# An SBUF-to-SBUF copy and transposes of the rounded type for the scaled attention scores

## The chip, the core and the metric

The kernel runs on one core of one Trainium2 chip. The metric is the device time of one execution in microseconds (us), as the median of several runs. Engines are named as in the profile: PE (TensorE, matrix products and transposes), PEld (its weight loads, which overlap PE), DVE (VectorE), ACT (ScalarE), POOL (GpSimd), SP (SyncE, which here only issues transfers). SBUF is the memory on the core, 128 partitions wide; PSUM holds the results of PE; DRAM is the large memory outside.

## What is computed

The reference is one layer of an encoder for two sequences (prompt and sample) of 1024 rows by 1024 columns, in fp32. The change lies in its attention part. Cut to that and its neighbours:

```python
h = rmsnorm(x, g_mix) * (1.0 + sc1) + sh1
z = h @ w_in                                   # 256 q_lat, 128 kv_lat, 64 k_pe, 512 f_in
q = (rmsnorm(q_lat, g_q_lat) @ w_uq)           # 4 heads of 128 + 64
q_pe, k_pe = apply_rope(q_pe), apply_rope(k_pe)
sc = (qn @ k_nope.T + q_pe @ k_pe.T) * scale   # per head, 1024 x 1024
p = jax.nn.softmax(sc, axis=-1)
y_mla = p @ v
mix = jnp.concatenate([y_mla, y_four], axis=-1) @ w_out
x = x + ga1 * mix
h2 = rmsnorm(x, g_ffn) * (1.0 + sc2) + sh2
ffn = (jax.nn.silu(h2 @ w_gate) * (h2 @ w_up)) @ w_down
out = rmsnorm(x + ga2 * ffn, g_final)
```

`y_four` is a Fourier mixing of the 512 columns of `f_in`. It is done before attention begins.

## The kernel before, in words

**Arithmetic.** An fp32 product is made of three products in the rounded type F32R (the trace prints `fp32r`). `split` (L61 to L63) turns a tile into a rounded high part (ACT, L62) and the rest (DVE, L63). `mm3` (L82 to L85) multiplies high by high, high by low and low by high. A plain fp32 tile can go through PE as well, which the kernel does only for transposes. A transpose on PE is a product with a 128 x 128 identity matrix: `ident` in fp32, `identr` in the rounded type. `rd(t)` (L58) reads the bits of a rounded tile as fp32.

**Stages.** Up to about 300 us of the span run the modulation, the input projection and the Fourier part. From 300 to 722 us runs attention (L1175 to L1338), and from there to the end the feed-forward part with products of the Strassen kind (`bank` in the profile). The rest of this section is on attention.

**Items.** Attention is cut into 64 items (s, b, h, u): 2 sequences, 4 blocks of 256 queries, 4 heads, 2 halves of 128 queries. Eight items make a block. Item k runs like this:

1. PE makes the scores of 128 queries against 1024 keys (`scores`, L1186 to L1200) into `ps_s`, two PSUM tiles of 1024 columns: for each 512 columns three products of the absorbed query `qa` with the latent keys `lat` (L1191 to L1193), and products with the rotary query `qp` (L1194, L1199, L1200).
2. DVE takes the maximum of each row (L1206, `mx`) and multiplies it by the negative scale (L1207, `nb`).
3. ACT takes the exponential from PSUM into the SBUF tile `p` (L1209), with the sum of each row.
4. DVE takes the reciprocal of the sum (L1210, `rr`) and scales `p` in place (L1211).
5. In the next item's turn PE turns `p` (`flip_p`, L1215 to L1226): eight transposes of 128 x 128 (L1225) in two groups of four, each group into one PSUM tile `ppt`. ACT and DVE split it into `pt`.
6. After every fourth item `values` (L1228) multiplies `pt` by the values `ckv`, 24 products, for two heads.

Between these stand, for the block ahead: `load_q` (L819, loads `ql`), `rope_q` (L834, the rotary query, with a temporary of 512 columns from `half`, L808, tag "hv"), `rope_flip` (L855, its transposes in the rounded type at L858), `absorb_q` (L863, the absorbed query `qa`, from `qa_tiles`, L831). And for the block behind: `out_load` (L1117, loads the tile `x2`, which the profile prints as `x`), `out_proj` (L1123, 12 products for 512 columns of output), `norm2` (L1132: stores `x2`, squares it on ACT, makes the reciprocal root `rs_r` on POOL by `rstd`, L100, and scales on DVE at L1143 into `xn`), `flip_h` (L1150: transposes of `xn` at L1157 into `pht`, shift and scale on ACT at L1160, and a store of `ht` at L1162).

**Memory.** A tile of a pool is given a number of buffers by `bufs`; the next tile of that tag waits until the one that many tiles ago is no longer read. Before the change `p` has three buffers, `qa` three, `hv` two. The PSUM tiles of the transposes (`tbank`, L1114: `ppt`, `pht`, `pqt`) share two.

**Order.** The Python code says what is done item by item (the loop from L1290 on, with `todo`, L1283, for the smaller steps). The framework's scheduler then sets the order of each engine, by its own estimates, so one more instruction in a chain can move others on every engine. Each engine goes through its list in order: an instruction that waits holds up all behind it.

**Transfers.** SP issues the loads and most stores of this stage, in one list: `ql`, `lat`, `ckv`, `x2`, `ht`, and at the change of sequence, items 34 to 38, the gate `gah` (L1244, in `gate_half`) and the weights `wvr` (L1269, in `wv_load`), which POOL multiplies by the gate (L1270). POOL issues transfers that add into DRAM (`add_x`, L798). When attention ends the next stage loads its input `H` from DRAM (L1366 and L1376), issued by SP as well.

Of the kernel before, what the change touches and what calls it, by code (L numbers as in the profile page):

```python
# [12 lines left out]
F32 = mybir.dt.float32  # L13
F32R = mybir.dt.float32r
# [7 lines left out]
P = 128  # L22
D = 1024
N = 1024
# [28 lines left out]
def hybrid_encoder_kernel(ctx: ExitStack, tc: tile.TileContext, a: dict):  # L53
    nc = tc.nc
# [3 lines left out]
    def rd(t):  # L58
        return t.bitcast(F32)

    def split(hi, lo, src):  # L61
        here["a"] = nc.scalar.copy(hi, src).ins  # L62
        here["v"] = nc.vector.tensor_tensor(out=lo, in0=src, in1=rd(hi), op=ALU.subtract).ins  # L63
# [27 lines left out]
    ident = const.tile([P, P], F32, name="ident")  # L91
    make_identity(nc, ident)
    identr = const.tile([P, P], F32R, name="identr")
# [81 lines left out]
    with ExitStack() as st:  # L175
        p1b = st.enter_context(ExitStack())
        w2 = p1b.enter_context(tc.tile_pool(name="p1b", bufs=1, side="right", reuse_waits="tile"))
        w = st.enter_context(tc.tile_pool(name="p1", bufs=1, reuse_waits="tile"))
# [617 lines left out]
    S = {}  # L796
# [9 lines left out]
            nc.gpsimd.dma_start(fo_d[s][bs, gs], xs[s][bs, gs], accum_op=ALU.add)  # L806

    def half(name):  # L808
        return e.tile([P, 512], F32, tag="hv", name=name, bufs=2)

    def load_seq(s, lat):
        ckv = [e.tile([P, 8, KVL], F32R, tag=f"ckv{i}", name=f"ckv{i}", bufs=1) for i in range(2)]
# [16 lines left out]
        return e.tile([P, HEADS, P], F32R, tag="qp", name="qp", bufs=4)  # L829

    def qa_tiles():  # L831
        return [e.tile([P, 256], F32R, tag=f"qa{i}", name=f"qa{i}", bufs=3) for i in range(2)]

    def rope_q(s, b, u, bankf):  # L834
        ql = S["q", s, b]
# [27 lines left out]
    def absorb_q(s, b, h, bankf):  # L863
        ql = S["q", s, b]
        pq = bankf()
        hs = slice(h * P, h * P + P)
        for c in range(2):
            mm3(pq[:, :256], wq_h[:, c, hs], wq_l[:, c, hs], ql[0][:, c, :], ql[1][:, c, :], c == 0, c == 1)
        qa = qa_tiles()
        split(qa[0], qa[1], pq[:, :256])  # L870
        S["qa", s, b, h] = qa

    def stage3_loads():
        wq_h = e.tile([P, 2, 768], F32R, name="wq_h")
        wq_l = e.tile([P, 2, 768], F32R, name="wq_l")
        half("hv")
        rc = e.tile([P, 8, ROPE], F32, name="rc")
        rs = e.tile([P, 8, ROPE], F32, name="rs")
        lat = [e.tile([P, 2, N], F32R, tag=f"lat0{i}", name=f"lat0{i}") for i in range(2)]
        sk_tile()  # L880
        load_q(0, 0)
        for c in range(2):
            wqr = e.tile([P, 768], F32, tag=f"ckv{c}", name="wqr", bufs=1)
            nc.sync.dma_start(wqr, wq_d[:, c])
            split(wq_h[:, c, 512:768], wq_l[:, c, 512:768], wqr[:, 512:768])
            split(wq_h[:, c, 0:512], wq_l[:, c, 0:512], wqr[:, 0:512])
        qa_tiles()
        nc.sync.dma_start(rc, a["ropec"])
        nc.sync.dma_start(rs, a["ropes"])
        load_seq(0, lat)  # L890
        return wq_h, wq_l, rc, rs

    with ExitStack() as st:
        early = st.enter_context(ExitStack())
        wa = early.enter_context(tc.tile_pool(name="p2a", bufs=1, reuse_waits="tile"))
        w = st.enter_context(tc.tile_pool(name="p2", bufs=1, side="right", reuse_waits="tile"))
# [175 lines left out]
        for s in range(2):  # L1072
            for n in range(8):
                g, j = n // 4, (1, 2, 3, 0)[n % 4]
# [14 lines left out]
                if s == 1 and n == 0:  # L1089
# [3 lines left out]
                    e = E3.enter_context(tc.tile_pool(name="p3e", bufs=1, side="left", reuse_waits="tile"))  # L1093
# [20 lines left out]
    def tbank(name, dt=F32):  # L1114
        return tl_ps.tile([P, 4, P], dt, tag="t", name=name, bufs=2)
# [59 lines left out]
    with ExitStack() as st:  # L1175
        w = st.enter_context(tc.tile_pool(name="p3", bufs=1, side="right", reuse_waits="tile"))
# [3 lines left out]
        def score_bank():  # L1180
            return pp.tile([P, N], F32, tag="s", name="ps_s", bufs=2)

        def scores(s, b, h, u):
            lat = S[s][0]
            qa, qp = S["qa", s, b, h], S["qp", s, b, u]
            us = slice(u * P, u * P + P)  # L1186
            ps = score_bank() if u == 0 else S.pop("ps")
            for g in range(2):
                gs = slice(512 * g, 512 * g + 512)
                o = ps[:, gs]  # L1190
                nc.tensor.matmul(o, qa[0][:, us], lat[0][:, 0, gs], start=u == 0, stop=False)  # L1191
                nc.tensor.matmul(o, qa[0][:, us], lat[1][:, 0, gs], start=False, stop=False)
                nc.tensor.matmul(o, qa[1][:, us], lat[0][:, 0, gs], start=False, stop=False)  # L1193
                nc.tensor.matmul(o, qp[:, h, :], lat[0][:, 1, gs], start=False, stop=u == 1)  # L1194
            if u == 0:
                pn, qn = score_bank(), S["qp", s, b, 1]
                for g in range(2):
                    gs = slice(512 * g, 512 * g + 512)
                    nc.tensor.matmul(ps[:, gs], qp[:64, h, :], lat[1][:64, 1, gs], start=False, stop=True)  # L1199
                    nc.tensor.matmul(pn[:, gs], qn[64:, h, :], lat[1][64:, 1, gs], start=True, stop=False)  # L1200
                S["ps"] = pn
            mx = tiny.tile([P, 1], F32, name="mx")
            nb = tiny.tile([P, 1], F32, name="nb")
            sm = tiny.tile([P, 1], F32, name="sm")
            rr = tiny.tile([P, 1], F32, name="rr")
            nc.vector.tensor_reduce(out=mx, in_=ps, axis=AX.X, op=ALU.max)  # L1206
            here["nb"] = nc.vector.tensor_scalar(out=nb, in0=mx, scalar1=-SCALE, scalar2=None, op0=ALU.mult).ins  # L1207
            p = w.tile([P, N], F32, tag="p", name="p", bufs=3)
            here["exp"] = nc.scalar.activation(p, ps, AF.Exp, bias=nb, scale=SCALE, accum_out=sm).ins  # L1209
            nc.vector.reciprocal(rr, sm)  # L1210
            nc.vector.tensor_scalar(out=p, in0=p, scalar1=rr[:, 0:1], scalar2=None, op0=ALU.mult)  # L1211
            S["p", s, b, h, u] = p
            S["rr"] = rr

        def flip_p(s, b, h, u):  # L1215
            p = S.pop(("p", s, b, h, u))
            if h % 2 == 0 and u == 0:
                S["pt", s, b, h // 2] = [[w.tile([P, 4, 4, P], F32R, tag=f"pt{k}{g}", name=f"pt{k}{g}", bufs=1) for k in range(2)]
                                         for g in range(2)]
            i = 2 * (h % 2) + u  # L1220
            for g in range(2):
                pth, ptl = S["pt", s, b, h // 2][g]
                pt = tbank("ppt")
                for c in range(4):
                    nc.tensor.transpose(pt[:, c, :], p[:, (4 * g + c) * P : (4 * g + c + 1) * P], ident)  # L1225
                split(pth[:, :, i, :], ptl[:, :, i, :], pt)  # L1226

        def values(s, b, q):  # L1228
            ckv = S[s][1]
# [66 lines left out]
        for k in range(nit + 4):  # L1296
            if k >= nit:
                i = k - nit
# [5 lines left out]
            if k < nit:  # L1304
                s, b, h, u = items[k]
                scores(s, b, h, u)
                if "scale" in S:
                    with tc.issue_after(here["nb"]):
                        S.pop("scale")()
                if k == nit - 1:  # L1310
                    with tc.issue_after(here["exp"]):
                        nc.scalar.activation(tiny.tile([P, 1], F32, tag="pc", name="warm"), cmask[:, 0:1], AF.Silu)
                nxt = items[k + 8 - k % 8] if k + 8 - k % 8 < nit else None
                i = k % 8
                if nxt is not None:
                    if i == 0:
                        load_q(*nxt[:2])
                    if i == 3 and nxt[1] == 0:
                        load_seq(nxt[0], [w.tile([P, 2, N], F32R, tag=f"lat1{i}", name=f"lat1{i}") for i in range(2)])
                    if i in (3, 4):  # L1320
                        rope_q(*nxt[:2], i - 3, gbank)
                    if i in (5, 6):
                        rope_flip(*nxt[:2], i - 5, tbank("pqt", F32R))
                if u == 1 and k + 1 < nit:
                    absorb_q(*items[k + 1][:3], gbank)
# [4 lines left out]
            if 0 <= k - 1 < nit:  # L1330
                flip_p(*items[k - 1])
                if k == nit:
                    S["tail"] = here["a"], here["v"]
# [6 lines left out]
    with ExitStack() as st:  # L1340
        w = st.enter_context(tc.tile_pool(name="p5", bufs=1, reuse_waits="tile"))
# [170 lines left out]
        for s in range(2):  # L1512
# [243 lines left out]
            def first_squares(half, t, v):  # L1756

                m[half, t] = tiny.tile([P, 2], F32, name=f"ms_{half}")
                me[half, t] = tiny.tile([P, 1], F32, name=f"me_{half}")
                jk = val()  # L1760
                nc.scalar.activation(jk, v, AF.Square, scale=1.0 / 32.0, accum_out=m[half, t][:, 0:1])
                nc.gpsimd.tensor_scalar(out=me[half, t], in0=m[half, t][:, 0:1], scalar1=EPS, scalar2=None, op0=ALU.add)
# [217 lines left out]
```

## Time and profile before

| | before |
|---|---|
| time, median of 3 runs | 2027.19 us (2027.05 to 2034.22) |
| time of the profiled execution | 2031.3 us |
| its span in the trace | 2029.5 us |
| instructions in the trace | 28291 |
| busy of PE, 0 to 300 us | 283.69 of 300 us |
| busy of PE, 300 to 722 us (attention) | 412.87 of 422 us |
| busy of PE, 722 to 2029 us | 1287.65 of 1307 us |
| mean granted clock of PE | 0.994 |

The profile is of one execution. Its times in the trace count from the start of the span. In a row of the timeline stand the start, the time that the group of like instructions took (for a group of several, from the first to the end of the last), the engine, the line of the kernel, the operation, its tiles as "out <- in", the shape, and the count; a bracket at the end holds the time that the engine idled ahead of it and what it waited for. In the groups, "busy, mean ns of one" is followed by the idle time ahead of the group and what ended it. Durations of products on PE overlap, since a product starts while the one ahead drains; how fast PE gets on is read from the starts. SPq and POOLq are the lists of transfers of SP and POOL.

### The profile page before, as it was taken

To read this page: it belongs to the slowest core of one execution; us is meant where nothing else is said; L and a number is where in the kernel's file an instruction comes from. 1 tells how busy PE (TensorE), PEld (TensorE's weight loads), DVE (VectorE), ACT (ScalarE), POOL (GpSimd) and SP (SyncE) were. 2 spreads that over 40 slices of the span, in tenths; PEclk is the share of its full clock that TensorE was granted. 3 is DMA by queue.
4 is the path that set the end of the run, shared out by engine and by line. 5 is a ranking of instruction groups with operands and counts; after the bars stand their busy time and mean duration, and the time that the engine had idled before them with its cause. 6 is when DMAs were issued, how large, how long until landed. Compare 5 with 4: busy or idle time off the path is not lost.

```text
span 2029.5 us, 28291 instructions
## 1 busy us (share of the span) xinstructions
PE 1984.2 (98%) x9840; PEld 1624.1 (80%) x9840; DVE 1407.3 (69%) x2088; ACT 896.9 (44%) x1733; POOL 830.1 (41%) x1013
## 2 busy tenths in 40 slices
PE   8899999999999999999999999999999999999997
PEld 7788877888777777888888888877788888888876
DVE  5667757766677679878677577687755655657674
ACT  4555545555555564333333365453333333336441
POOL 2454123112313227879779411233654555510142
PEclk9999999999999999999999999999999999999999
DMA  9685793445542575645655587674422322357662
GB/s 376 207 289 171 255 346 102 125 94 130 138 122 94 178 269 187 207 163 192 206 166 190 178 304 249 219 234 147 141 93 102 116 93 103 116 184 270 229 224 89
DMA packets 181963, 370.33 MB, mean 182 GB/s; under 512 B 18556, under 2 KB 58236, under 8 KB 177724
## 3 DMA queue, kind: packets, MB, share of 16 engines
q1 hardware_dynamic: 163148, 310.71, 45.8%
q0 software_dynamic: 18672, 57.81, 9.5%
q8 instruction: 77, 1.26, 0.3%
q14 instruction: 66, 0.54, 0.1%
HBM read 256.46 MB, written 120.39 MB: 186 GB/s over the span
## 4 chain that ended last, share of the span: by engine, by line
PE 54%; DVE 2%; DMA 2%; POOL 1%; issue 1%; ACT 1%; SPq 0%; DVEq 0%; ACTq 0%; POOLq 0%
PE bank L84 18%; PE bank L83 18%; PE bank L85 18%; DVE wl L63 1%; DMA draw<-s_d 1%; POOL val L143 1%; DVE val L143 1%; ACT wh L62 0%; DMA val<-x_d 0%; DMA draw<-t_d 0%; DVE val L1777 0%; POOL rs_y L110 0%; DMA rgu<-in_wgu_dram 0%; DVE val L1751 0%; DVE val L140 0%
## 5 line engine op out<-in xcount | busy, mean ns | idle before, releaser
L83 PE MATMUL bank<-H,wh 128*128 128x512 f32 x1224 | 477.3, 390 | 5.1 <-DVE val L143 5.1
L85 PE MATMUL bank<-H,wl 128*128 128x512 f32 x1224 | 476.3, 389 | 0.2 <-DVE wl L63 0.2
L84 PE MATMUL bank<-H,wh 128*128 128x512 f32 x1224 | 476.2, 389 | 0.0
L143 DVE TENSOR_TENSOR val<-bank,val 128x512 f32<-128x512 f32 x244 | 166.8, 688 | 169.9 <-PE bank L85 167.2
L83 PEld LDWEIGHTS bank<-H,wh 128*128 128x128 f32 x1224 | 229.8, 188 | 55.6 <-DVE val L143 7.0
L85 PEld LDWEIGHTS bank<-H,wl 128*128 128x128 f32 x1224 | 229.8, 188 | 49.2 <-DVE wl L63 1.1
L84 PEld LDWEIGHTS bank<-H,wh 128*128 128x128 f32 x1224 | 229.8, 188 | 47.3
L63 DVE TENSOR_TENSOR wl<-draw,wh 128x512 fp32r<-128x512 f32 x286 | 201.3, 739 | 83.0 <-ACT wh L62 82.4
L62 ACT CAST wh<-draw 128x512 fp32r<-128x512 f32 x286 | 168.6, 621 | 157.9 <-PE bank L84 86.8
L84 PE MATMUL bank<-wl,wh 128*128 128x512 f32 x572 | 223.6, 391 | 2.5 <-DVE wl L63 2.5
L143 POOL TENSOR_TENSOR val<-val 128x512 f32<-128x512 f32 x58 | 83.1, 1441 | 344.9 <-DVE val L1751 188.7
L85 PE MATMUL bank<-wh,wl 128*128 128x512 f32 x572 | 222.6, 389 | 0.0
L83 PE MATMUL bank<-wh 128*128 128x512 f32 x572 | 222.6, 389 | 0.0
L62 ACT CAST wh<-rgu 128x512 fp32r<-128x512 f32 x171 | 106.5, 624 | 249.1 <-PE bank L84 193.8
L63 DVE TENSOR_TENSOR wl<-val,wh 128x512 fp32r<-128x512 f32 x133 | 132.4, 997 | 75.5 <-ACT wh L62 75.4
L63 DVE TENSOR_TENSOR wl<-rgu,wh 128x512 fp32r<-128x512 f32 x171 | 168.1, 984 | 5.8 <-ACT wh L62 5.8
L62 ACT CAST wh<-val 128x512 fp32r<-128x512 f32 x133 | 82.4, 623 | 178.7 <-PE bank L84 162.8
L140 POOL TENSOR_TENSOR val<-rgu 128x512 f32<-128x512 f32 x80 | 113.1, 1414 | 96.4 <-DMA rgu<-in_wgu_dram 92.6
L84 PEld LDWEIGHTS bank<-wl,wh 128*128 128x128 f32 x572 | 107.4, 188 | 27.7 <-DVE wl L63 5.5
L83 PEld LDWEIGHTS bank<-wh 128*128 128x128 f32 x572 | 107.4, 188 | 22.7 <-ACT wh L62 0.2
L85 PEld LDWEIGHTS bank<-wh,wl 128*128 128x128 f32 x572 | 107.4, 188 | 21.7
L140 POOL TENSOR_TENSOR val<-val 128x512 f32<-128x512 f32 x89 | 119.4, 1358 | 1.3
(393 smaller groups left out, 3919.9 us busy)
## 6 DMA issues: line engine op xcount, KB each, us to landing
rgu<-in_wgu_dram SPq DMA_DIRECT2D x86, 512.0 KB
draw<-s_d SPq DMA_DIRECT2D x143, 256.0 KB
s_d<-val POOLq DMA_DIRECT2D x88, 256.0 KB, 3.9
draw<-t_d SPq DMA_DIRECT2D x88, 256.0 KB
s_d<-val SPq DMA_DIRECT2D x66, 256.0 KB
wada<-in_wa_dram SPq DMA_DIRECT2D x16, 1024.0 KB
draw<-in_w_down_dram SPq DMA_DIRECT2D x55, 256.0 KB
xt<-in_x_dram SPq DMA_DIRECT2D x16, 512.0 KB
```

The costliest lines, as they stand in the source:

```text
L62: here["a"] = nc.scalar.copy(hi, src).ins
L63: here["v"] = nc.vector.tensor_tensor(out=lo, in0=src, in1=rd(hi), op=ALU.subtract).ins
L83: nc.tensor.matmul(out, lh, rh, start=first, stop=False, skip_group_check=cont)
L84: nc.tensor.matmul(out, lh, rl, start=False, stop=False, skip_group_check=cont)
L85: here["pe"] = nc.tensor.matmul(out, ll, rh, start=False, stop=last, skip_group_check=cont).ins
L140: return eng.tensor_tensor(out=out, in0=x, in1=y, op=ALU.subtract).ins
L143: return eng.tensor_tensor(out=out, in0=x, in1=y, op=ALU.add).ins
```

## The change

Three tags lose a buffer: `hv` goes from two to one, `qa` from three to two, `p` from three to two. A new tile `pr` of the same size as `p`, of the rounded type and with two buffers, is filled from `p` by a transfer that SP issues after the scaling (`rd(pr)` makes it a copy of bits, so nothing is rounded in it). The eight transposes read `pr` with `identr` and write PSUM tiles declared in the rounded type, whose bits `split` reads as fp32. Two lines are added, so the transposes stand at L1227 in the kernel after, and what lies behind L1212 moves by two lines too.

```diff
     def half(name):
-        return e.tile([P, 512], F32, tag="hv", name=name, bufs=2)
+        return e.tile([P, 512], F32, tag="hv", name=name, bufs=1)
...
     def qa_tiles():
-        return [e.tile([P, 256], F32R, tag=f"qa{i}", name=f"qa{i}", bufs=3) for i in range(2)]
+        return [e.tile([P, 256], F32R, tag=f"qa{i}", name=f"qa{i}", bufs=2) for i in range(2)]
...
-            p = w.tile([P, N], F32, tag="p", name="p", bufs=3)
+            p = w.tile([P, N], F32, tag="p", name="p", bufs=2)
             here["exp"] = nc.scalar.activation(p, ps, AF.Exp, bias=nb, scale=SCALE, accum_out=sm).ins
             nc.vector.reciprocal(rr, sm)
             nc.vector.tensor_scalar(out=p, in0=p, scalar1=rr[:, 0:1], scalar2=None, op0=ALU.mult)
-            S["p", s, b, h, u] = p
+            pr = w.tile([P, N], F32R, tag="pr", name="pr", bufs=2)
+            nc.sync.dma_start(rd(pr), p)
+            S["p", s, b, h, u] = pr
             S["rr"] = rr
...
             for g in range(2):
                 pth, ptl = S["pt", s, b, h // 2][g]
-                pt = tbank("ppt")
+                pt = tbank("ppt", F32R)
                 for c in range(4):
-                    nc.tensor.transpose(pt[:, c, :], p[:, (4 * g + c) * P : (4 * g + c + 1) * P], ident)
-                split(pth[:, :, i, :], ptl[:, :, i, :], pt)
+                    nc.tensor.transpose(pt[:, c, :], p[:, (4 * g + c) * P : (4 * g + c + 1) * P], identr)
+                split(pth[:, :, i, :], ptl[:, :, i, :], rd(pt))
```

How the change moves instructions, on PE and in SP's list of transfers, is shown by rows of both orders. On PE, at the item that follows the two absorbed-query products (`wq_h` and `wq_l` are weights, `gb` their PSUM tile), before:

```order
L85 MATMUL gb<-ql_4207,wq_l 128x256
L1225 MATMUL ppt<-ident,p 128x128 x8
L1191 MATMUL ps_s<-lat_3470,qa_4962 128x512
L1192 MATMUL ps_s<-lat_3471,qa_4962 128x512
L1193 MATMUL ps_s<-lat_3470,qa_4963 128x512
```

and after the change:

```order
L85 MATMUL gb<-ql_4225,wq_l 128x256
L1191 MATMUL ps_s<-lat_3470,qa_5002 128x512
L1227 MATMUL ppt<-identr,pr 128x128 x8
L1192 MATMUL ps_s<-lat_3471,qa_5002 128x512
L1193 MATMUL ps_s<-lat_3470,qa_5003 128x512
```

The transposes have moved behind the first product of the next scores. On PE, at the item whose transposes stand beside an output projection (`gb<-wv`) and the last transposes of `xn`, before:

```order
L85 MATMUL gb<-ql_4741,wq_l 128x256
L1157 MATMUL pht<-ident,xn 128x128 x4
L1225 MATMUL ppt<-ident,p 128x128 x4
L83 MATMUL gb<-wv_3745,o0b_4546 128x512
L84 MATMUL gb<-wv_3746,o0b_4546 128x512
```

and after the change:

```order
L1157 MATMUL pht<-ident,xn 128x128 x4
L84 MATMUL gb<-wv_3746,o0b_4574 128x512
L85 MATMUL gb<-wv_3745,o1b_4575 128x512
L83 MATMUL gb<-wv_3745,o0b_4574 128x512
L84 MATMUL gb<-wv_3746,o0b_4574 128x512
L85 MATMUL gb<-wv_3745,o1b_4575 128x512
L83 MATMUL gb<-wv_3745,o0b_4574 128x512
L84 MATMUL gb<-wv_3746,o0b_4574 128x512
L85 MATMUL gb<-wv_3745,o1b_4575 128x512
L83 MATMUL gb<-wv_3745,o0b_4574 128x512
L84 MATMUL gb<-wv_3746,o0b_4574 128x512
L1227 MATMUL ppt<-identr,pr 128x128 x8
```

One more such product (L83) stands ahead of `pht` there, so eleven of the twelve products of the projection now come before the transposes, which come as one group of eight. In SP's list at the change of sequence, before (`h_d` and `x_d` are DRAM tiles):

```order
L1162 DMA h_d_104<-ht 128x4x128
L1269 DMA wvr_6087<-wo_d 128x512 x2
L1269 DMA wvr_6351<-wo_d 128x512 x3
L1244 DMA gah<-ga_d 128x512
L1135 DMA x_d_99<-x_5567 128x1024
L1120 DMA x_6157<-fo_d_97 128x1024
```

and after the change:

```order
L1162 DMA h_d_104<-ht 128x4x128 x2
L1271 DMA wvr_6157<-wo_d 128x512 x3
L1213 DMA pr<-p 128x1024
L1271 DMA wvr_6157<-wo_d 128x512
L1271 DMA wvr_6427<-wo_d 128x512 x2
L1213 DMA pr<-p 128x1024
L1246 DMA gah<-ga_d 128x512
L1135 DMA x_d_99<-x_5623 128x1024
L1213 DMA pr<-p 128x1024
L1120 DMA x_6229<-fo_d_97 128x1024
```

Three of the copies stand between these transfers, two of them ahead of the gate `gah`.

## The prediction

> **What bounds the kernel now.** The page comes first: its table of engines says that TensorE (PE) is busy for nearly the whole span, and its list of the costliest groups that matrix products in splits of three fill it.
>
> ```profile
> PE 1984.2 (98%) x9840; PEld 1624.1 (80%) x9840; DVE 1407.3 (69%) x2088; ACT 896.9 (44%) x1733; POOL 830.1 (41%) x1013
> ```
>
> A mean over stages hides where the change lies. The list by source of L1225, the transposes of the scaled scores, gives their shortest, median and longest duration in ns and the first and last start:
>
> ```profile
> L1225 PE MATMUL ppt<-ident,p x512: 270/273/447, 309.5 to 721.5; 128*128 128x128 f32 x171
> ```
>
> The table by windows of 300 to 722 us has, by column, the window, its length, the busy times of PE, PEld (weight loads), DVE, ACT and POOL with their counts, the granted clock, the share of DMA and GB/s.
>
> ```profile
> 300.00:350.00 50.00, 45.15 (x243) 34.51 (x241) 36.66 (x68) 24.22 (x47) 15.28 (x14) 0.93 0.41 122
> ...
> 500.00:550.00 50.00, 48.99 (x269) 39.67 (x267) 32.37 (x62) 26.21 (x56) 18.68 (x28) 1.00 0.67 174
> ...
> sum 422.00, PE 412.87 PEld 330.70 DVE 295.91 ACT 229.22 POOL 97.71; mean PE 45.87 PEld 36.74 DVE 32.88 ACT 25.47 POOL 10.86
> ```
>
> TensorE idles 422.00 - 412.87 = 9.1 us of this stage, over half of it in the first 50 us, where the clock fell to 0.93 as well. DVE and ACT have room. The list of waits of PE in the same window says what ended the three longest:
>
> ```profile
> PE ps_s L1191 <- ACT qa L62: 2.8, 1, 2.8
> PE pht L1157 <- DVE pt L63: 1.9, 1, 1.9
> PE ppt L1225 <- DVE nb L1207: 1.9, 1, 1.9
> ```
>
> So every nanosecond that an instruction takes on TensorE here is on the path, and so is every wait that is put in front of it, but no wait elsewhere is. The change does both: shorter transposes, and a transfer between the scaled scores and the transposes.
>
> **What it takes away: the pace of the transposes.** The groups by form give count, busy time and mean of the old transposes (L1225) and of the rotary ones that already use the rounded type (L858):
>
> ```profile
> L1225 PE MATMUL ppt<-ident,p 128*128 128x128 f32 x512 | 73.0, 279 | 3.3 <-DVE nb L1207 1.9 <-DVE pt L63 0.9 <-ACT ht L1160 0.5
> L1225 PEld LDWEIGHTS ppt<-ident,p 128*128 128x128 f32 x512 | 57.4, 142 | 20.5 <-ACT ht L1160 6.7 <-issue 6.4 <-ACT qp L860 2.0
> L858 PEld LDWEIGHTS pqt<-identr,qsk 128*128 128x128 f32 x56 | 5.9, 141 | 3.3 <-issue 2.6
> ```
>
> Durations overlap, so the pace is read from starts. Two stretches of the timeline hold the same things, a product of 512 columns, eight transposes and another such product: full fp32 first, rounded second.
>
> ```profile
> 409.90 0.39 PE L85 MATMUL gb<-pt,ckv 128*128 128x512 f32 x1
> 410.13 1.03 PE L1225 MATMUL ppt<-ident,p 128*128 128x128 f32 x8
> 410.92 0.48 PE L1191 MATMUL ps_s<-lat,qa 128*128 128x512 f32 x1
> 411.24 0.40 PE L1192 MATMUL ps_s<-lat,qa 128*128 128x512 f32 x1
> ```
>
> ```profile
> 296.50 0.40 PE L85 MATMUL bank<-wm,B 128*128 128x512 f32 x1
> 296.73 0.81 PE L858 MATMUL pqt<-identr,qsk 128*128 128x128 f32 x8
> 297.38 0.47 PE L83 MATMUL bank<-wm,A 128*128 128x512 f32 x1
> 297.68 0.40 PE L84 MATMUL bank<-wm,A 128*128 128x512 f32 x1
> ```
>
> From the first product to the one behind the next it is 411.24 - 409.90 = 1.34 us against 297.68 - 296.50 = 1.18 us: 0.16 us less for eight. There are 512 / 8 = 64 such groups: 64 x 0.16 = 10.2 us less, all on the path. This is the whole direct gain, and nearly a ceiling.
>
> [...]
>
> A smaller gain: where two groups of four stood with one product between, the second waited for a free bank.
>
> ```profile
> 340.60 0.47 PE L1191 MATMUL ps_s<-lat,qa 128*128 128x512 f32 x1
> 341.05 0.66 PE L1225 MATMUL ppt<-ident,p 128*128 128x128 f32 x4
> ```
>
> Start to start that is 0.45 us where a product takes about 0.23 us (410.13 - 409.90). The order now has two products there; at about seven such places up to 7 x 0.22 = 1.5 us goes.
>
> **What it adds: 64 transfers in the chain.** Nothing in the trace copies SBUF to SBUF. The nearest rows of the DMA issues (last number: median us from issue to landing) are:
>
> ```profile
> fo_d<-in_x_dram POOLq DMA_DIRECT2D x16, 512.0 KB, 7.5
> hc_d<-val POOLq DMA_DIRECT2D x16, 256.0 KB, 2.9
> x_d<-x POOLq DMA_DIRECT2D x3, 512.0 KB, 3.7
> ```
>
> A copy of 512 KB out of SBUF takes 3.7 us when POOL issues it, half of that 2.9 us; an accumulating transfer of the size takes 7.5 us. I take 2.9 us for a copy that SP issues into SBUF, and 2.3 to 4.4 us as its ends, since neither POOL's issuing nor a landing in DRAM is in it. [...]
>
> Does it fit? The scheduler moved transposes later. By the rows of PE's order above, at the item whose transposes follow the two absorbed-query products, one product of about 0.23 us has moved ahead of them. In the trace of before this item scales its scores and turns them at:
>
> ```profile
> 417.16 0.75 DVE L1211 TENSOR_SCALAR p<-p,rr 128x1024 f32<-128x1024 f32 x1
> ...
> 420.55 1.04 PE L1225 MATMUL ppt<-ident,p 128*128 128x128 f32 x8
> ```
>
> The slack is 420.55 - 417.91 = 2.64 us; with the product moved in it is 2.87, less 0.16 for the shorter group of the item ahead: 2.7 us against 2.9. A wait of 0.2 us, in seven blocks of eight items: 1.4 us. The two other tight places of a block:
>
> ```profile
> 422.46 0.78 DVE L1211 TENSOR_SCALAR p<-p,rr 128x1024 f32<-128x1024 f32 x1
> 426.49 0.66 PE L1225 MATMUL ppt<-ident,p 128*128 128x128 f32 x4
> ...
> 444.61 0.75 DVE L1211 TENSOR_SCALAR p<-p,rr 128x1024 f32<-128x1024 f32 x1
> 446.54 0.60 PE L1225 MATMUL ppt<-ident,p 128*128 128x128 f32 x4
> ```
>
> The first has 426.49 - 423.24 = 3.25 us, nothing moved: it fits. The second has 446.54 - 445.36 = 1.18 us, and by the second pair of PE's rows above eleven products of out_proj now stand ahead of its transposes, 11 x 0.23 = 2.5 us: 3.7, it fits. The other five items of a block have over 2.6 us or a values step ahead of them.
>
> The copies also stand in SP's queue, where each waits for its scaling and holds what is behind it: loads of x2 and ql, stores of h2, and at the change of sequence the weights wvr and the gate gah. By the rows of SP's order above the gate now stands behind two copies. What hung on it before:
>
> ```profile
> 510.33 0.32 SPq L1244 DMA_DIRECT2D gah<-ga_d  x1
> ...
> 513.68 5.03 POOL L1270 TENSOR_TENSOR wvr<-wvr,gah 128x512 f32<-128x512 f32 x4 [3.38 <-DMA gah<-ga_d]
> ...
> 520.80 0.76 DVE L1143 TENSOR_SCALAR xn<-x,rs_r 128x1024 f32<-128x1024 f32 x1 [5.92 <-POOL rs_r L114]
> 521.66 0.78 DVE L1211 TENSOR_SCALAR p<-p,rr 128x1024 f32<-128x1024 f32 x1
> ...
> 523.69 1.25 PE L1225 MATMUL ppt<-ident,p 128*128 128x128 f32 x8 [0.88 <-DVE pt L63]
> ```
>
> The gate frees POOL, POOL the norm (L1143), the norm the scaling in DVE's order, and that the transposes: 523.69 - 522.44 = 1.25 us of slack. The gate comes about 1 us later and the copy takes 2.9: 1.0 + 2.9 - 1.25 = 2.6 us of wait, once.
>
> Copies beside other transfers take longer: the windows show a DMA share of 0.41 and 0.67. I allow some ten of 64 copies 0.4 us of wait beyond their slack: 4 us, with 0 and 12 as ends. In the first 50 us the stalls (2.8 and 1.9 above) hang on POOL's products and stay; 0 there, -3 to +3. At the end the loads of the next stage stand behind the last two copies, where before they were long under way:
>
> ```profile
> 702.42 1.02 SPq L1366 DMA_DIRECT2D H<-h_d  x2
> ...
> 722.29 2.01 ACT L62 CAST H<-H 128x1024 fp32r<-128x1024 f32 x2
> ```
>
> They had 20 us of room, and lose most of it: 0.5 us, ends 0 and 2. The smaller pools (hv, qa, p) cost 0: the order shows no operation of the chain moved for them, and without that cover qa's third buffer could cost a wait like the 2.8 us above.
>
> The sum: -10.2 - 1.5 + 1.4 + 2.6 + 4 + 0.5 = -3.2 us. The profiled execution took 2031.3 us (its span is 2029.5), so by it 2028.1; the median of the three runs, 2027.19, is 4.1 lower, and 2027.19 - 3.2 = **2024.0 us**.
>
> **The rivals.** First, the copy is hidden everywhere. The order speaks for it: every tight place got more cover or had 2.6 us. With a copy of 2.3 us all waits but 1 us are gone: 2027.2 - 11.7 + 1 = 2016.5 us. Against it speak the three rows of landings.
>
> Second, slower: the copy takes the place of the transposes as what PE waits for. It decides at a copy of about 3.5 us, where the gain per block is used up. At 4.4 us the item of 2.7 us of slack waits 1.7 us (the one of 3.25 behind it gains that much slack, and waits for nothing), the one of 3.7 us 0.7 and the one behind it an estimated 0.4: 2.8 us a block, 20 us in seven, 4.1 at the gate and 6 beside other transfers: -11.7 + 30 = +18, 2045 us. For it: 3.7 us for the same size. Against it: that row contains POOL's issue.
>
> Third, the pace does not change, because in this loop a weight load limits both: the loads are equally long (142, 141). Then +8.5, 2035.7 us. Against: the two stretches above.
>
> [...]
>
> **How the numbers follow.** The forecast has 0.66, its own range 2017.5 to 2033; the hidden copy 0.14, the slow copy 0.12, the unchanged pace 0.06, the short loads 0.02. 0.5%, about what a measurement of this kernel can tell from no change, is 10.1 us: below 2017.1 or above 2037.3. Faster: most of the hidden copies (0.11) and the short loads: 0.13. Slower: the slow copy from 3.9 us on (0.09) and one in four of the unchanged pace (0.02): 0.11. The rest, 0.76, is the same. The range for 8 in 10 takes in the hidden copy and part of the slow one: 2014.5 to 2037.
>
> **What would show it.** In the profile after, the transposes of L1227 have stretches of 1.18 us as above; PE waits for the copy at the item behind the absorbed queries by about 0.2 us a block and by 2 to 3 us once near 523; the list of waits names the DMA pr<-p with some 8 us in all; idle in the stage is near 15 us. The sum is wrong if that list shows under 3 us or over 20, or if the stretch of eight is 1.34 us.

## The result and the profile after

The changed kernel took 2106.07 us (median of 4 runs, 2102.89 to 2108.14) beside 2030.7 us for the kernel before in the same comparison: 1.0367 times as long, with a 95% interval of 1.0335 to 1.0400. The prediction had 2024.0 us, in a range of 2014.5 to 2037.0.

The page's table of engines for the kernel after shows PE's share of the span down from 98% to 95%, in a span of 2106.4 us:

```profile
PE 2005.9 (95%) x9840; PEld 1633.1 (78%) x9840; DVE 1419.0 (67%) x2088; ACT 896.3 (43%) x1733; POOL 830.5 (39%) x1013
```

PE was idle for 2106.4 - 2005.9 = 100.5 us, and before for 2029.5 - 1984.2 = 45.3: 55 us more. It was also busy for 2005.9 - 1984.2 = 21.7 us more, though its transposes had become shorter. Both are in the attention stage, as the table by windows shows (length, busy time of each engine, then clock, share of DMA and GB/s):

```profile
300.00:797.00 497.00, 433.56 (x2268) 340.58 (x2268) 303.08 (x541) 229.38 (x470) 97.26 (x157) 0.93 0.56 171
797.00:2106.00 1309.00, 1288.12 (x5667) 1058.60 (x5665) 919.99 (x1123) 506.02 (x888) 626.53 (x628) 1.00 0.53 181
```

The stage was 422 us long and is 497; the rest of the kernel took 1307 us and takes 1309. Of the 75 us, 54.3 are idle time (63.4 against 9.1) and 20.7 are busy time (433.56 against 412.87), at a granted clock of 0.93 where it was 0.99. The list of waits of PE in the stage names the transfer (us in total, times, longest):

```profile
PE ppt L1227 <- DMA pr<-p: 52.4, 16, 6.6
```

The prediction said that the sum is wrong if this list shows over 20 us for the copy. It shows 52.4. Yet most copies are quick. One that had SP to itself, by the timeline of the kernel after (scaling, issue of the copy, transposes):

```profile
415.94 0.76 DVE L1211 TENSOR_SCALAR p<-p,rr 128x1024 f32<-128x1024 f32 x1
...
416.76 0.47 SPq L1213 DMA_DIRECT2D pr<-p  x1
...
420.01 0.79 PE L1227 MATMUL ppt<-identr,pr 128*128 128x128 f32 x8
```

From the issue to the transposes pass 3.25 us, and PE waited for nothing there. And one two items on:

```profile
428.43 0.34 SPq L1120 DMA_DIRECT2D x<-fo_d  x1
...
428.46 0.79 DVE L1211 TENSOR_SCALAR p<-p,rr 128x1024 f32<-128x1024 f32 x1
...
428.64 1.01 POOL L806 DMA_DIRECT2D fo_d<-in_x_dram  x1
...
429.31 0.47 SPq L1213 DMA_DIRECT2D pr<-p  x1
...
439.12 1.23 PE L1227 MATMUL ppt<-identr,pr 128*128 128x128 f32 x8 [5.41 <-DMA pr<-p]
```

Here 9.8 us pass, 5.41 of them as idle time of PE. Two transfers stand just ahead of this copy: a load of `x2` in SP's own list, issued 0.88 us before it, and from POOL an adding transfer of 512 KB (`add_x`, L806), issued 0.67 us before it. The load alone does little: in the kernel without adding transfers (below) the copy of this item stands 0.88 us behind the same load and lands in 3.98 us, where it takes 9.67 here. By the trace's records of where each copy ended, 23 of the 64 landed within 3.1 us of their issue and 19 took 5.7 to 10.0 us; 18 of these 19 ran beside one of the sixteen adding transfers, and the last one beside a store of 1 MB that POOL issues and two loads of SP.

That is no chance. `add_x` releases its transfer by a small sum of `rr` (L804), and `rr` is what the scaling waits for too, so both start within a microsecond of each other by construction. It was there to be read in the timeline of before, beside the very scalings that the prediction quotes (417.16 and 422.46):

```profile
417.92 0.88 POOL L806 DMA_DIRECT2D fo_d<-in_x_dram  x1
...
422.73 0.89 POOL L806 DMA_DIRECT2D fo_d<-in_x_dram  x1
```

### The profile page after: what moved, and what is told of

It reads as the page before. It is cut to its first block, busy times and chain, and to the rows that moved or that the text cites. A ratio compares the mean times of both kernels' runs of the same rounds, so it can differ in the third digit from the quotient of the medians.

```text
span 2106.4 us, 28590 instructions
## 1 busy us (share of the span) xinstructions
PE 2005.9 (95%) x9840; PEld 1633.1 (78%) x9840; DVE 1419.0 (67%) x2088; ACT 896.3 (43%) x1733; POOL 830.5 (39%) x1013
## 3 DMA queue, kind: packets, MB, share of 16 engines
q8 instruction: 77, 1.26, 0.2%
## 4 chain that ended last, share of the span: by engine, by line
PE 51%; DVE 3%; DMA 2%; issue 1%; POOL 1%; ACT 1%; SPq 0%; DVEq 0%; ACTq 0%; POOLq 0%
PE bank L83 17%; PE bank L84 17%; PE bank L85 17%; DVE wl L63 1%; DMA draw<-t_d 1%; ACT wh L62 1%; DVE val L143 1%; DMA draw<-s_d 1%; POOL val L143 0%; DVE val L1779 0%; DMA rgu<-in_wgu_dram 0%; POOL rs_y L110 0%; DVE val L1753 0%; DMA val<-x_d 0%; DMA draw<-in_w_down_dram 0%
## 5 line engine op out<-in xcount | busy, mean ns | idle before, releaser
L83 PE MATMUL bank<-H,wh 128*128 128x512 f32 x1224 | 477.4, 390 | 5.9 <-DVE val L143 5.4
L83 PEld LDWEIGHTS bank<-H,wh 128*128 128x128 f32 x1224 | 229.7, 188 | 57.1 <-DVE val L143 7.1
L83 PE MATMUL bank<-wh 128*128 128x512 f32 x572 | 222.8, 389 | 0.4 <-ACT wh L62 0.4
L143 POOL TENSOR_TENSOR val<-val 128x512 f32<-128x512 f32 x58 | 82.4, 1429 | 343.8 <-DVE val L1753 189.6
L83 PEld LDWEIGHTS bank<-wh 128*128 128x128 f32 x572 | 107.4, 188 | 23.5 <-ACT wh L62 1.0
L63 DVE TENSOR_TENSOR pt<-ppt,pt 128x512 fp32r<-128x512 f32 x128 | 83.7, 683 | 58.1 <-ACT pt L62 57.7
```

Source lines behind the costliest of these rows:

```text
L83: nc.tensor.matmul(out, lh, rh, start=first, stop=False, skip_group_check=cont)
L143: return eng.tensor_tensor(out=out, in0=x, in1=y, op=ALU.add).ins
```

## The experiments

Theory A, collision: the adding transfers hold the copies, because they start at the same moment, and PE pays for it in waiting and again in clock. Theory B, the copy itself: a transfer in this chain costs its wait, whatever else moves. Rivals for parts of it were the smaller pools (C), the mere traffic of the copies (T) and the clock (K).

| kernel | us, median | ratio to before, 95% interval |
|---|---|---|
| after | 2106.07 | 1.0367 (1.0335 to 1.0400) |
| after, no adding transfers | 2045.52 | 1.0079 (1.0064 to 1.0094) |
| before, no adding transfers | 2034.0 | 1.0011 (1.0002 to 1.0021) |
| adding transfers at every fourth item | 2111.44 | 1.0402 (1.0386 to 1.0417) |
| adding transfers when the copy has landed | 2081.11 | 1.0248 (1.0231 to 1.0265) |
| adding transfers halved, at four items a block | 2090.8 | 1.0288 (1.0273 to 1.0304) |
| PE kept busy in the long waits | 2119.42 | 1.0437 (1.0415 to 1.0458) |
| before, smaller pools | 2031.89 | 1.0012 (1.0003 to 1.0022) |
| before, smaller pools and copies that nobody reads | 2039.73 | 1.0039 (1.0026 to 1.0052) |
| no copy, scores rounded by the scaling | 2020.89 | 0.9953 (0.9939 to 0.9968) |
| the same, without the products that this makes zero | 1990.16 | 0.9801 (0.9785 to 0.9818) |

### No adding transfers

```diff
         with tc.issue_after(place):
-            nc.gpsimd.dma_start(fo_d[s][bs, gs], xs[s][bs, gs], accum_op=ALU.add)
+            pass
```

> The kernel after, without the sixteen adding transfers of L806 (the input x is left out of the result). Theory A, collision: these transfers start within 1 us of a copy pr<-p, move 512 KB each and hold the copy for some 5 us; without them the copies land in 2.9 to 5 us, the waits of L1227 for pr<-p fall from 52 us to under 15, and the granted clock of 0.86 to 0.97 in the stage rises to near 1; the time is 2018 to 2040 us. Theory B, the copy itself: wherever a copy stands in the chain it costs the wait, whatever else moves; the time stays at 2080 to 2110 us.

It took 2045.52 us: 60.6 of the 75 us are gone. PE's waits in the stage:

```profile
PE ppt L1227 <- DMA pr<-p: 11.7, 8, 4.7
```

52.4 us of waiting became 11.7, as theory A has it, and of the 19 copies of 5.7 us and more three are left. Theory B's 2080 to 2110 is out. The time is 5 us above the upper end that A was given, so copies in the chain cost something by themselves as well. The largest wait left, 4.7 us, stands near the end of the stage, where the copy is issued between two loads of `hca` (512 KB each) and 0.33 us behind a store of 1 MB that POOL issues:

```profile
666.46 0.33 SPq L1252 DMA_DIRECT2D hca<-h_d  x1
...
666.73 0.65 POOL L1262 DMA_DIRECT2D hc_d<-hcb  x1 [0.30 <-POOL hcb L140]
...
667.06 0.47 SPq L1213 DMA_DIRECT2D pr<-p  x1
...
667.58 0.58 SPq L1252 DMA_DIRECT2D hca<-h_d  x1
...
674.38 0.72 PE L1227 MATMUL ppt<-identr,pr 128*128 128x128 f32 x4 [4.68 <-DMA pr<-p]
```

The same edit to the kernel before:

> The kernel before without the sixteen adding transfers (x is left out of the result). Theory A: they cost nothing where no copy stands in the chain, 2026 to 2033 us, and what their removal gave after the change was all collision. If they have a price of their own: below 2020 us.

2034.0 us, against 2030.73: no gain, rather 0.4 to 4.3 us more, and 1 us above the range that theory A was given. So the adding transfers are free where nothing in the chain moves at the same time. The 60.6 us belong to the meeting of the two.

One rival has to be set aside. Without the adding transfers the scheduler also changed the order: 163 of the 9840 places in PE's list and 42 of the 2088 in DVE's hold another instruction than after. But the kernel with halved adding transfers (below) has the same lists on PE, DVE and ACT as the one without, by the two traces (SP's differ at 3 places), and it takes 2090.8 us. So the order isn't what gained the 60 us.

### Other places for the adding transfers

At every fourth item:

```diff
-        for i, k in enumerate((6, 8, 10, 12, 17, 18, 19, 25, 26, 27, 33, 34, 35, 41, 42, 43)):
+        for i, k in enumerate(range(0, 64, 4)):
```

> The kernel after, with the same sixteen adding transfers at every fourth item (0, 4, 8 to 60), the items that have 7 to 8 us between scaling and transposes. Theory A: a copy held for 5 us fits there, so most waits go; the copies of the items next to them may still be touched; 2025 to 2060 us, under 25 us of waits for pr<-p. Theory B: nothing changes, 2095 to 2115 us.

2111.44 us, with 57.4 us of waits for the copy: a miss for theory A, and inside the range given to theory B. PE, DVE and ACT have the same order as after. The timeline of this kernel shows what happened at one such place:

```profile
424.45 0.99 POOL L806 DMA_DIRECT2D fo_d<-in_x_dram  x1
...
426.88 0.34 SPq L1135 DMA_DIRECT2D x_d<-x  x1
...
431.01 0.75 DVE L1211 TENSOR_SCALAR p<-p,rr 128x1024 f32<-128x1024 f32 x1
...
434.98 0.34 SPq L1120 DMA_DIRECT2D x<-fo_d  x1
...
435.43 0.47 SPq L1213 DMA_DIRECT2D pr<-p  x1
```

The copy of this item did fit. But now the adding transfer meets the store of `x2` (426.88), and the next load of `x2`, which reuses that buffer, waits for the store until 434.98. In SP's list the next item's copy stands behind that load: scaled at 431.76, it is issued only at 435.43, 0.45 us behind 512 KB of load. In SP's waits in the stage the load of `x2` waited 46.9 us for `x_d<-x`, and 21.3 us for the adding transfers themselves, which write the rows that it reads. The collision had moved from the copy to the store and the load, and reached the copies by SP's order.

So another item alone doesn't part the two. With the old items, released by the copy's landing:

```diff
-        place = nc.gpsimd.tensor_tensor(out=pc, in0=S["rr"], in1=S["rr"], op=ALU.add).ins
+        place = nc.gpsimd.tensor_tensor(out=pc, in0=S["land"], in1=S["land"], op=ALU.add).ins
...
-            S["rr"] = rr
+            S["rr"], S["land"] = rr, rd(pr)[:, 0:1]
```

> The kernel after, with the sixteen adding transfers at their old items, but issued only when the item's copy has landed (POOL's small sum that releases them reads pr in place of rr). Theory A, collision in time: the copy of the same item now lands in 2.9 to 5 us; the next item's copy, issued 5 to 7 us later, still meets the last 2 to 4 us of the adding transfer. The waits for pr<-p fall from 52 to 15 to 35 us, and the time to 2055 to 2085 us. Theory B, the copy itself: 2095 to 2115 us.

2081.11 us, inside theory A's 2055 to 2085, with the rest of the program in the same order on PE, DVE and SP:

```profile
PE ppt L1227 <- DMA pr<-p: 33.5, 15, 5.4
```

What is left is only in part what was expected. At four items (the 8th, 20th, 28th and 44th, waits of 3.1 to 4.7 us) the next item's copy does meet the adding transfer, but 1.6 to 2.4 us behind its issue and not 5 to 7, and takes 6.7 to 8.0 us. The longest wait, 5.4 us, is a copy that was scaled at 392.15 us and issued at 395.50, behind a load of `x2` that waited 7.6 us for an adding transfer which writes its rows. Another, of 4.6 us, is the one between the loads of `hca`.

Half the size, 32 pieces at items 0, 1, 4 and 5 of each block:

```diff
-        s, b, g = i // 8, i // 2 % 4, i % 2
-        bs = slice(256 * b, 256 * b + 256)
+        s, b, g = i // 16, i // 2 % 8, i % 2
+        bs = slice(128 * b, 128 * b + 128)
...
-        for i, k in enumerate((6, 8, 10, 12, 17, 18, 19, 25, 26, 27, 33, 34, 35, 41, 42, 43)):
+        for i, k in enumerate(8 * n + j for n in range(8) for j in (0, 1, 4, 5)):
```

> The kernel after, with the adding transfers cut in two (128 rows of 512 columns, 256 KB, 32 in all) and put at items 0, 1, 4 and 5 of each block, whose transposes come 4.4 to 8.2 us after the scaling. Theory A: what a collision costs is how long the adding transfer lasts less the slack of the place; half the size holds a copy or a store some 2 to 3 us, and most copies land within 6 us: waits for pr<-p under 25 us, 2050 to 2075 us. If every adding transfer costs its wait whatever its size (32 of them): 2100 us or more.

2090.8 us, with 38.5 us of waits for the copy: better than after, but outside both ranges, and over the 25 us given to theory A. Its list by source of L806 and one place of its timeline:

```profile
DMA to landing us min/median/max: 4.6/6.2/8.7
```

```profile
422.07 0.93 POOL L806 DMA_DIRECT2D fo_d<-in_x_dram  x1 [0.26 <-issue]
...
423.03 0.34 SPq L1120 DMA_DIRECT2D x<-fo_d  x1
...
423.50 0.47 SPq L1213 DMA_DIRECT2D pr<-p  x1
...
431.12 1.23 PE L1227 MATMUL ppt<-identr,pr 128*128 128x128 f32 x8 [4.34 <-DMA pr<-p]
```

Half the bytes don't take half the time: 6.2 us at the median, where the whole ones after took 8.8 by the same list. And at seven of the items 1 and 5 three transfers start within 2.2 us: the piece, a load of `x2` and the copy.

### The clock behind a wait

Twelve items waited over 2.6 us in the kernel after. Ahead of their transposes stands work for PE that nobody needs:

```diff
+                for j in range(WARM.get(32 * s + 8 * b + 2 * h + u, 0) if g == 0 else 0):
+                    nc.tensor.transpose(pt[:, j % 4, :], identr, identr)
                 for c in range(4):
```

with `WARM = {3: 18, 6: 28, 8: 40, 10: 24, 17: 50, 19: 40, 25: 50, 26: 20, 34: 62, 41: 30, 42: 26, 53: 40}`.

> The kernel after, with 18 to 62 transposes of the identity ahead of the transposes of the twelve items that waited over 2.6 us (428 in all, some 37 us of PE's time, sized to end 1 us before the copy lands). Theory K, clock: the slow stretch of 4 to 6 us behind each such wait comes from the idle time before it; with PE busy the granted clock stays at 1.0 and 15 to 30 us go, 2076 to 2092 us, though work was added. Rival: only the wait itself counts, and the work is hidden in it: 2100 to 2112 us; or the work isn't hidden: over 2115 us.

2119.42 us: a miss. The mechanism is there, its gain isn't. At the item shown above (428.46) the kernel after goes on like this, in PE's timeline, from the first to the last of twelve products of the output projection and the product behind them:

```profile
440.14 0.76 PE L83 MATMUL gb<-wv,o0b 128*128 128x512 f32 x1
...
444.96 0.51 PE L85 MATMUL gb<-wv,o1b 128*128 128x512 f32 x1
445.31 0.39 PE L1191 MATMUL ps_s<-lat,qa 128*128 128x512 f32 x1
```

Twelve products take 445.31 - 440.14 = 5.17 us, 0.43 us each. With PE busy through the wait (lines there are one or two higher):

```profile
440.40 4.50 PE L1228 MATMUL ppt<-identr 128*128 128x128 f32 x50
444.93 0.86 PE L1230 MATMUL ppt<-identr,pr 128*128 128x128 f32 x8
445.63 0.47 PE L84 MATMUL gb<-wv,o0b 128*128 128x512 f32 x1
...
448.47 0.39 PE L1192 MATMUL ps_s<-lat,qa 128*128 128x512 f32 x1
```

they take 448.47 - 445.63 = 2.84 us, 0.24 each. The trace's records of the granted clock say the same: 0.5 from 438.37 to 445.20 us in the kernel after, 1.0 all through these rows here. So the slow stretch does come from the idle time before it, and costs some 2.3 us at this place. But where PE came earlier to the next held copy, it waited there. Ten items on, in this kernel's timeline:

```profile
529.50 0.72 PE L1230 MATMUL ppt<-identr,pr 128*128 128x128 f32 x4 [4.45 <-DMA pr<-p]
```

The kernel after turned the same scores at 529.54 without a wait: 4.45 us ahead became a wait of 4.45 us. The added work also moved other instructions, and near the end a copy came to stand among loads of `hca`:

```profile
771.47 1.23 PE L1230 MATMUL ppt<-identr,pr 128*128 128x128 f32 x8 [7.27 <-DMA pr<-p]
```

That wait of 7.27 us was 0.89 us in the kernel after. In all of attention the time that PE was busy at a clock of 0.5 fell only from 55.6 to 37.8 us. The total therefore doesn't price the clock; the stretch of twelve products does.

### Pools, unread copies, direct scaling

The kernel before with `hv` 1, `qa` 2 and `p` 2 buffers:

> The kernel before with only the three smaller pools (hv 1, qa 2, p 2). Theories A and B: nothing waits for these buffers, 2027 to 2034 us. Rival C, buffers: a good part of the loss is theirs, over 2045 us.

2031.89 against 2029.49 us, 0.6 to 4.5 us by the interval. The smaller pools are nearly free, and C is out.

The same with the copies, which nobody reads:

```diff
             nc.vector.tensor_scalar(out=p, in0=p, scalar1=rr[:, 0:1], scalar2=None, op0=ALU.mult)
+            pr = w.tile([P, N], F32R, tag="pr", name="pr", bufs=2)
+            nc.sync.dma_start(rd(pr), p)
             S["p", s, b, h, u] = p
```

> The kernel before with the smaller pools and the 64 copies pr<-p, which nobody reads: the transposes turn p in fp32 as before. Theory A: a copy costs only what the transposes wait for it, so 2027 to 2040 us. Rival T, traffic: the copies hold up the loads and stores behind and beside them enough to matter by themselves: 2050 to 2090 us.

2039.73 us, 9 us above before (5 to 11 by the interval), of which some 2.4 are the pools'. Traffic (T) is not what costs 75 us. What it does cost has a visible part, in this kernel's timeline at the change of sequence:

```profile
522.92 1.27 POOL L1272 TENSOR_TENSOR wvr<-wvr,gah 128x512 f32<-128x512 f32 x1
...
524.93 0.75 DVE L1143 TENSOR_SCALAR xn<-x,rs_r 128x1024 f32<-128x1024 f32 x1 [9.03 <-POOL rs_r L114]
...
525.78 0.78 DVE L1211 TENSOR_SCALAR p<-p,rr 128x1024 f32<-128x1024 f32 x1
...
527.82 1.97 PE L1227 MATMUL ppt<-ident,p 128*128 128x128 f32 x8 [4.37 <-DVE pt L63]
```

This is the prediction's chain from the late gate over POOL and the norm to the transposes, with 4.37 us of idle time where before had 0.88 and the kernel with the smaller pools alone 1.18. These transposes don't read the copy, so it comes by SP's list and the traffic, not by a wait for the copy. These copies meet the adding transfers too, but nothing waits for them.

Scaling straight into `pr`:

```diff
-            nc.vector.tensor_scalar(out=p, in0=p, scalar1=rr[:, 0:1], scalar2=None, op0=ALU.mult)
             pr = w.tile([P, N], F32R, tag="pr", name="pr", bufs=2)
-            nc.sync.dma_start(rd(pr), p)
+            nc.vector.tensor_scalar(out=pr, in0=p, scalar1=rr[:, 0:1], scalar2=None, op0=ALU.mult)
```

> The kernel after without its 64 copies: DVE scales straight into pr, so the scores are rounded there and their low part is lost; buffers and rounded transposes as after. The prediction's direct gain, 0.16 us for each of 64 groups of eight, and 1.5 us at the banks: 2015 to 2022 us beside 2030.7. If the pace of the transposes doesn't count here: 2028 to 2034. If the smaller pools cost something: above 2034.

2020.89 us against 2029.49, 6.5 to 12.4 us less by the interval: the gain of the rounded transposes is real, and the copy ate it. It beats both kernels, at the price of scores rounded to the short type. Rounded scores have no low part, so its split and a third of the values products only move zeros. Without them:

```diff
-                split(pth[:, :, i, :], ptl[:, :, i, :], rd(pt))
+                here["a"] = here["v"] = nc.scalar.copy(pth[:, :, i, :], rd(pt)).ins
...
-                mm3(po, ckv[0][:, c, :], ckv[1][:, c, :], pth, ptl, c == 0, c == 7)
+                nc.tensor.matmul(po, ckv[0][:, c, :], pth, start=c == 0, stop=False)
+                here["pe"] = nc.tensor.matmul(po, ckv[1][:, c, :], pth, start=False, stop=c == 7).ins
```

> The kernel with the scaling straight into pr (no copy, scores rounded there), and without what the rounding makes zero: no low part of the turned scores, so one copy on ACT in place of the split, and 16 products in place of 24 in each of the 16 values steps. By the row of about 0.23 us a product, 16 x 8 x 0.23 = 29 us less than the direct kernel's 2021, if PE stays the bound: 1988 to 1998 us. If DVE or the chain of the softmax takes over in the shorter items: 2000 to 2015 us.

1990.16 us, 1.8 to 2.2% under before by the interval, and as expected. PE is still the bound, at 1944.7 us busy of a span of 1985.4:

```profile
PE 1944.7 (98%) x9712; PEld 1591.4 (80%) x9712; DVE 1336.5 (67%) x1960; ACT 895.7 (45%) x1733; POOL 828.8 (42%) x1013
```

## Why the prediction was wrong

**The step that failed** is "I allow some ten of 64 copies 0.4 us of wait beyond their slack: 4 us, with 0 and 12 as ends". By the prediction PE's waits for the copy come to some 8 us in all, these 4 among them; the list of waits has 52.4, and 11.7 without the adding transfers. Taking these away gave 60.6 us. The prediction had the row of that transfer in hand (7.5 us to landing, longer than every slack that it listed within a block) and used it only as an end for what a copy takes. It took "beside other transfers" from the share of DMA, 0.41 and 0.67, a mean over 50 us. The mean says nothing about whether two transfers start in the same microsecond; L804 does.

Two things made the miss as large as it is. A held copy takes mostly 8 to 10 us (14 of the 18 beside an adding transfer), and not 0.4 more than alone: in the records the copy issued at 429.31 ended at 438.98, the adding transfer of 428.64 at 439.14. In all fifteen pairs issued 0.3 to 0.8 us apart the two ends lie within 1.3 us.

The trace's records of single packets show more. An undisturbed copy (issued at 416.76) moves its 128 packets from 1.1 to 2.4 us after its issue. Two copies that met an adding transfer and nothing else just ahead (512.77 and 643.03) moved the first one only after 4.3 and 4.5 us, when 127 and 144 of the adding transfer's 256 packets had started; from there the packets of both go on side by side, and the copies landed after 8.3 us. The one copy issued less than 0.1 us behind an adding transfer (568.77) moved its first packet ahead of the other's, and landed in 3.50 us. In the kernel with halved pieces it is the same, where SP has no load within a microsecond ahead: three copies issued 0.03 to 0.08 us behind a piece landed in 3.6 to 4.0 us, nine issued 0.6 to 0.7 us behind one in 5.2 to 5.9. So a few tenths of a microsecond at the issue decide. No run here shows why the first packet of a held copy comes so late.

And a long wait is paid for again in clock. The sum priced waits by their idle time and put the clock at nothing. Of the stage's 75 us more, 20.7 are busy time at the lower clock, and more than that if one counts that the transposes alone became shorter. By the records of the granted clock, PE was busy for 55.6 us of attention at a clock of 0.5, and before for 5.1; half of the difference, 25 us, is an estimate of what the clock cost.

In the kernel after, all twelve waits of PE on these transposes of 2.6 us and more are followed by 3.4 to 6.1 us at that clock, and none of those up to 2.2 us is. A product takes 0.43 us there, against 0.23 at a clock of 1.0. All stretches at 0.5 in this stage are 3.41, 6.83 or 10.24 us long and begin on one grid of 3.41 us. Four of the twelve waits (2.62, 2.78, 3.06 and 3.23 us) were shorter than one step of this grid.

Cut on that grid, the windows that start from 300 to 800 us in the traces of the twelve kernels show where the line lies. Of those at a clock of 1.0, all 55 in which PE idled for 1.8 us or more are followed by one at 0.5, none of the 1552 with under 1.1 us is, and in between 13 of 49 are.

**The other steps:**

- The pace of the transposes held. The same stretch as in the prediction, in the timeline of the kernel after:

```profile
402.20 0.39 PE L85 MATMUL gb<-pt,ckv 128*128 128x512 f32 x1
402.43 0.80 PE L1227 MATMUL ppt<-identr,pr 128*128 128x128 f32 x8
403.06 0.46 PE L1191 MATMUL ps_s<-lat,qa 128*128 128x512 f32 x1
403.36 0.39 PE L1192 MATMUL ps_s<-lat,qa 128*128 128x512 f32 x1
```

  403.36 - 402.20 = 1.16 us, where 1.18 was expected and 1.34 stood before. As a whole, 10.2 and 1.5 us were expected; the kernel without copies gained 8.6 against before, and 11.0 against the kernel that has only its smaller pools (2031.89). The third rival (pace unchanged) is out. The short loads, which were given a chance of 0.02, stand in no run: a weight load of these transposes takes 148 ns at the mean in the kernel after, where before it took 142.
- The single copy was sized right: 2.9 us, as the records of undisturbed ones have it. So was the slack of the tight places: without adding transfers no item from the eighth to the 52nd waited 1 us for its copy.
- The gate's chain was right in kind (2.6 us expected); in the kernel with unread copies its wait is 4.37 us, in the one without adding transfers 0.9, and that for the copy.
- The end of the stage (0.5 us, up to 2) came to 2 us, and the pools (0) to 2.4 (0.6 to 4.5): both small, as forecast.
- The second rival had the sign, at 0.12, and the wrong mechanism. It asked for copies that are slow everywhere (4.4 us), which they aren't; slow ones are tied to a partner.
- Within the steady blocks the copies then cost nothing, but the start of the stage, and a place near its end that the prediction didn't list, were wrong. Without adding transfers the kernel is 24.6 us slower than the one without copies (2045.5 against 2020.9). The transposes of three items, the seventh, the 49th and the 55th, start in the first of these two kernels at

```profile
354.64 1.26 PE L1227 MATMUL ppt<-identr,pr 128*128 128x128 f32 x8 [2.43 <-DMA pr<-p]
...
635.19 0.81 PE L1227 MATMUL ppt<-identr,pr 128*128 128x128 f32 x8
...
683.00 0.81 PE L1227 MATMUL ppt<-identr,pr 128*128 128x128 f32 x8
```

  and in the second at

```profile
342.88 0.51 PE L1227 MATMUL ppt<-identr,pr 128*128 128x128 f32 x4
...
624.19 0.81 PE L1227 MATMUL ppt<-identr,pr 128*128 128x128 f32 x8
...
660.66 0.54 PE L1227 MATMUL ppt<-identr,pr 128*128 128x128 f32 x4
```

  The difference is 11.8 us after the first block's loads of `wvr`, `gah` and `lat`, still 11.0 us 42 items later, and 22.3 us behind the copy that stood between the loads of `hca`. The prediction gave the start 0 us, -3 to +3. Of these 22 us, 5.0 lie ahead of the first transposes of all (316.64 against 311.65 us), and 11.5 are idle time of PE from there to the 55th item (18.4 against 6.9 us by the table of windows). The other 5.8 are busy time, an estimated 3.7 of it by the clock (14.1 against 6.8 us busy at 0.5, halved). Why the first transposes start later was not taken apart.

## What to carry to other kernels

Before a transfer is put into a chain that the bounding engine waits for, list what else is issued in the same microsecond and what releases it; with a shared releaser the collision comes back nearly every round (here 15 of the 16 copies issued just behind an adding transfer took 5.7 to 10.0 us, and one 3.5), and a mean share of DMA hides it. Price the chain at the length of the longest transfer that it can meet (here 7.5 us at the median before, 8.8 after), and follow SP's list from there: in the kernel with the adding transfers at every fourth item a held store held the load that reuses its buffer (46.9 us in the stage), and that load the copy behind it. Price a wait of TensorE of over some 2 us at about one and a half times its length, by an estimate from this case: here some 25 us of clock came with 54 us of idle time.

## What the runs showed that was not expected

- An adding transfer of 512 KB from DRAM to DRAM took 7.5 us at the median before and 8.8 after; one of 256 KB 6.2. A plain copy of 512 KB within SBUF, issued by SP, lands in 2.9 us.
- Work given to PE in a wait of 5.4 us kept its pace at 0.24 us a product where idling gave 0.43, and the whole was still no faster: where PE came earlier, it waited for the next transfer, and the added work was not all hidden.
- Whether a wait near 2 us is followed by half pace depends on where it falls: in the kernel with halved pieces one of 2.06 us was, and one of 2.23 us was not. The windows of the clock's grid around both, in the table by windows (length, busy time of each engine, then clock, share of DMA and GB/s):

```profile
397.80:401.21 3.41, 1.35 (x12) 1.20 (x12) 1.13 (x3) 1.35 (x3) 0.00 (x0) 1.00 0.45 165
401.22:404.63 3.41, 3.41 (x12) 2.73 (x12) 2.05 (x4) 2.14 (x6) 0.00 (x0) 0.50 0.09 37
...
524.10:527.51 3.41, 2.15 (x13) 1.20 (x11) 2.37 (x4) 0.64 (x2) 0.00 (x0) 1.00 0.87 219
527.51:530.92 3.41, 2.44 (x17) 2.12 (x18) 0.85 (x2) 1.91 (x4) 0.00 (x0) 1.00 0.02 6
```

  The first wait lies whole in one window, which has 3.41 - 1.35 = 2.06 us of idle time, and the next window runs at 0.5. The second is cut in two, 1.26 and 0.97 us, and the clock stays at 1.0.
